# Split-heads rotary embedding in f32: two programs aligned in the instruction stream, one wait moved, one copy cut in two

## The chip, the cores and the metric

The kernel runs on one core of one Trainium2 chip. The metric is the device time of one execution in microseconds (us). Before the change it is 162.48 us, the median of six runs from 162.23 to 162.66.

The core has five instruction streams, each in order: TensorE (PE: matmuls; its weight loads are shown as PEld), VectorE (DVE), ScalarE (ACT), GpSimd (POOL) and SyncE (SP). In this kernel SP issues all loads and stores. They go through one hardware queue (q1) to 16 DMA engines, each of which works through its share of the packets in order. Instructions themselves are fetched from memory too: the page lists such packets as queue q14, kind "instruction".

## The reference

The input x has shape (16, 512, 1024), 16 heads of 64, all f32. Every head is split in two halves, which are rotated by the cosine and sine of their position:

```python
batch, seq, dim = x.shape
head_dim = dim // num_heads
half_dim = head_dim // 2
x = x.reshape(batch, seq, num_heads, head_dim)
x1, x2 = (x[..., :half_dim].copy(), x[..., half_dim:].copy())
cos = cos[None, :, None, :].copy()
sin = sin[None, :, None, :].copy()
rotated = np.concatenate([x1 * cos - x2 * sin, x1 * sin + x2 * cos], axis=-1)
```

So each output element is one input element times a cosine plus its partner in the other half times a signed sine. 33.6 MB are read and 33.6 MB written.

## The kernel before

**Tiles.** Two batches make one tile of 128 partitions: a partition holds 8 rows (sequence positions) of 1024 elements, so a tile is 4 MB, and there are 8 tiles. Five tile buffers (pool xp) exist. The result of a tile is written over its input and stored from there.

**Loads and stores.** SP issues, in this order: rows 0 to 2 of tile 0, the sine and cosine tables, rows 3 to 7 of tile 0, tiles 1 to 4, and four tiny loads into a tile named spare that nothing reads (line 92). Then come the stores as tiles are done; behind the store of tile 2 it issues the loads of tiles 5, 6 and 7 (line 74), which wait until their buffers have been stored. The last tile is stored in two halves: rows 0 to 3, and rows 4 to 7 (LAST_OUT).

**Setting up.** GpSimd makes an identity matrix. VectorE clears a tile (line 97) that three matmuls use to clear the PSUM accumulators own_ps and pe_ps, and copies two identities side by side (spread, line 109). Two matmuls by spread (lines 113 and 114) put the tables on all partitions, and VectorE makes the signed sine table sns (lines 116 and 117) and its copy for row 0 (line 119).

**The rows of a tile are computed in three ways.**
- Row 0 (ROW_OWN): VectorE puts x times cosine into PSUM (own_ps, cos_product, line 141; this is done at the end of the tile before). Then own_product (line 150) multiplies the row in place by the sine, TensorE adds it to own_ps with halves swapped (pe_add, line 176), and ScalarE copies own_ps back over the row (line 209).
- Row 3 (ROW_PE): GpSimd makes the sine product b3 (line 165); VectorE makes the cosine product in PSUM, half a row at a time (pe_ps, line 141); TensorE adds, and ScalarE copies back (pe_half, line 181).
- The pairs of rows (1, 2), (4, 5) and (6, 7): GpSimd makes the sine product of both rows into a buffer b (sin_rows and sin_product, line 165), VectorE the cosine product into PSUM (pd, line 141), and VectorE adds the two over the rows (pair_sum, line 189).

GpSimd's buffers b come from a pool of three.

**The order** is that of the program: within tc.manual_schedule() nothing is moved. The framework finds from the memory that instructions touch which ones need a semaphore wait; it leaves out a wait that an earlier instruction of the same engine has already had. An instruction that needs more waits than it can carry gets separate wait instructions ahead of it, shown as EVENT_SEMAPHORE. Of the three 128x2048 sums of a tile each has one such instruction before it (24 in all, 21 ns each): a wait for VectorE's own product, beside the wait for GpSimd's b that the sum itself carries. Line 150 carries no wait.

Of the kernel before, what the change touches and what calls it, by code (L numbers as in the profile page):

```python
# [10 lines left out]
ALU = mybir.AluOpType  # L11
# [6 lines left out]
ROW_OWN, ROW_PE = 0, 3  # L18
# [10 lines left out]
def kernel(  # L29
# [13 lines left out]
    nc = tc.nc  # L43
# [20 lines left out]
    pd = ctx.enter_context(tc.tile_pool(name="pd", bufs=1, space=bass.MemoryType.PSUM))  # L64

    ctx.enter_context(tc.manual_schedule())

    tiles = [None] * NT

    def load(t, lo=0, hi=KK):  # L70
        if tiles[t] is None:
            tiles[t] = xp.tile([P, F], FP32, name="xt")
        s = slice(lo * dim, hi * dim)
        nc.sync.dma_start(out=tiles[t][:, s], in_=x_v[t][:, s])  # L74
# [23 lines left out]
    own_ps = pe.tile([P, dim], FP32)  # L98
    pe_ps = pe.tile([P, BANK], FP32)
    for ps in (own_ps[:, :BANK], own_ps[:, BANK:], pe_ps):  # L100
# [9 lines left out]
        out=spread.rearrange("p (b q) -> p b q", b=NB),  # L110
        in_=bass.AP(tensor=eye.tensor, offset=eye.offset, ap=[eye.ap[0], [0, NB], [1, PB]]),
# [9 lines left out]
    def heads(r):  # L121
        return r.rearrange("p (h a j) -> p h a j", a=2, j=half)

    def swapped(r):
        n = r.shape[1] // hd
        return bass.AP(tensor=r.tensor, offset=r.offset + half, ap=[r.ap[0], [hd, n], [-half, 2], [1, half]])

    def rows(t, k, n=1):
        return tiles[t][:, k * dim : (k + n) * dim]

    def cos_product(out, r, k, n=1):

        c = cos_t[:, k * half : (k + n) * half]
        m = r.shape[1] // (n * half)
        if n == 1:
            cb = bass.AP(tensor=c.tensor, offset=c.offset, ap=[c.ap[0], [0, m], [1, half]])
            o, i = (z.rearrange("p (a j) -> p a j", j=half) for z in (out, r))
        else:
            cb = bass.AP(tensor=c.tensor, offset=c.offset, ap=[c.ap[0], [half, n], [0, m], [1, half]])
            o, i = (z.rearrange("p (k a j) -> p k a j", k=n, j=half) for z in (out, r))  # L140
        nc.vector.tensor_tensor(out=o, in0=i, in1=cb, op=ALU.mult)  # L141

    def own_product(r):

        s = bass.AP(
            tensor=own_t.tensor,
            offset=own_t.offset + half,
            ap=[own_t.ap[0], [0, nh], [-half, 2], [1, half]],
        )
        nc.vector.tensor_tensor(out=heads(r), in0=heads(r), in1=s, op=ALU.mult)  # L150

    def sin_product(out, r, k, n):
        s = sns[:, k : k + n].rearrange("p k a j -> p (k a j)")
        if n == 1:
            sb = bass.AP(tensor=s.tensor, offset=s.offset, ap=[s.ap[0], [0, nh], [1, hd]])
            o, i = heads(out), swapped(r)
        else:
            sb = bass.AP(tensor=s.tensor, offset=s.offset, ap=[s.ap[0], [hd, n], [0, nh], [1, hd]])
            o = out.rearrange("p (k h a j) -> p k h a j", k=n, a=2, j=half)
            i = bass.AP(  # L160
                tensor=r.tensor,
                offset=r.offset + half,
                ap=[r.ap[0], [dim, n], [hd, nh], [-half, 2], [1, half]],
            )
        nc.gpsimd.tensor_tensor(out=o, in0=i, in1=sb, op=ALU.mult)  # L165

    def sin_rows(t, k, n):
        b = bp.tile([P, 2 * dim], FP32, name="b")[:, : n * dim]
        sin_product(b, rows(t, k, n), k, n)
        return b  # L170

    def parts(r):
        return [r[:, i * BANK : (i + 1) * BANK] for i in range(r.shape[1] // BANK)]

    def pe_add(ps, other):
        nc.tensor.matmul(out=ps, lhsT=ident, rhs=other, start=False, stop=True, skip_group_check=True)  # L176

    def pe_half(k, r, b):
        cos_product(pe_ps, r, k)
        pe_add(pe_ps, b)  # L180
        nc.scalar.copy(out=r, in_=pe_ps)  # L181

    def pair_product(t, k):
        ps = pd.tile([P, 2 * dim], FP32, name="pd")
        cos_product(ps, rows(t, k, 2), k, 2)
        return ps, rows(t, k, 2)

    def pair_sum(ps, r, b):
        nc.vector.tensor_tensor(out=r, in0=ps, in1=b, op=ALU.add)  # L189

    def stores(t):
        lo = 0
        for hi in LAST_OUT if t == NT - 1 else (KK,):
            store(t, lo, hi)
            lo = hi
        if t + 1 == NT - BUFS:
            for n in range(BUFS, NT):
                load(n)

    cos_product(own_ps, rows(0, ROW_OWN), ROW_OWN)  # L200
    for t in range(NT):
        first, second, third = PAIRS
        b1 = sin_rows(t, first[0], 2)
        p1 = pair_product(t, first[0])
        r0 = rows(t, ROW_OWN)
        own_product(r0)
        for ps, r in zip(parts(own_ps), parts(r0)):
            pe_add(ps, swapped(r))
        nc.scalar.copy(out=r0, in_=own_ps)  # L209
        b3 = sin_rows(t, ROW_PE, 1)  # L210
        b2 = sin_rows(t, second[0], 2)
        pair_sum(*p1, b1)
        h0, h1 = zip(parts(rows(t, ROW_PE)), parts(b3))
        pe_half(ROW_PE, *h0)
        p2 = pair_product(t, second[0])
        b1 = sin_rows(t, third[0], 2)
        pair_sum(*p2, b2)
        pe_half(ROW_PE, *h1)
        p1 = pair_product(t, third[0])
        if t + 1 < NT:  # L220
            cos_product(own_ps, rows(t + 1, ROW_OWN), ROW_OWN)
        pair_sum(*p1, b1)
        stores(t)
# [35 lines left out]
```

## Time and profile before

| | |
|---|---|
| median of six runs | 162.48 us (162.23 to 162.66) |
| the profiled execution | 162.66 us |
| its span, first to last instruction | 160.9 us |
| PE busy | 58.6 us, 36% of the span |
| VectorE busy | 136.3 us, 85% |
| ScalarE busy | 18.4 us, 11% |
| GpSimd busy | 127.2 us, 79% |
| DMA | 67.25 MB, 418 GB/s over the span |
| granted TensorE clock, mean | 0.648 of full speed |

The groups of instructions that the change touches, with count and mean duration:

| line, engine | what | count | mean ns |
|---|---|---|---|
| 165 GpSimd | sine product of two rows, 128x2048 | 24 | 4527 |
| 165 GpSimd | sine product of one row, 128x1024 | 8 | 2356 |
| 150 VectorE | own product, 128x1024 | 8 | 1213 |
| 189 VectorE | sum of a pair, 128x2048 | 24 | 2287 |
| 209 ScalarE | copy of own_ps, 128x1024 | 8 | 1012 |
| 181 ScalarE | copy of pe_ps, 128x512 | 16 | 586 |

The share of busy time is an average over the whole span. Engines work at the same time, so busy times are not added up; what sets the end is read from the chain of waits, from what still runs in the last microseconds, and from who waits for whom. A start and a duration are in us of the span's own clock. The trace also holds one record for each DMA packet, with its start, duration, size and queue.

### The profile page before, as it was taken

To read this page: it belongs to the slowest core of one execution; us is meant where nothing else is said; L and a number is where in the kernel's file an instruction comes from. 1 tells how busy PE (TensorE), PEld (TensorE's weight loads), DVE (VectorE), ACT (ScalarE), POOL (GpSimd) and SP (SyncE) were. 2 spreads that over 40 slices of the span, in tenths; PEclk is the share of its full clock that TensorE was granted. 3 is DMA by queue.
4 is the path that set the end of the run, shared out by engine and by line. 5 is a ranking of instruction groups with operands and counts; after the bars stand their busy time and mean duration, and the time that the engine had idled before them with its cause. 6 is when DMAs were issued, how large, how long until landed. Compare 5 with 4: busy or idle time off the path is not lost.

```text
span 160.9 us, 443 instructions
## 1 busy us (share of the span) xinstructions
PE 58.6 (36%) x71; PEld 19.6 (12%) x71; DVE 136.3 (85%) x85; ACT 18.4 (11%) x25; POOL 127.2 (79%) x38
## 2 busy tenths in 40 slices
PE   3041915055503731191309250745047402922000
PEld 0111301021102210131003010211022101310000
DVE  1059969999999999999999999999999999998000
ACT  0001311003000301011100310031003010211000
POOL 1039999999999999988998899898999899840000
PEclk9999995558555775568555955585557655685555
DMA  5999999999999999999999999999999999999993
GB/s 192 394 423 457 416 489 399 391 505 407 391 505 408 391 424 489 391 399 505 401 399 489 407 399 497 407 399 489 407 399 497 407 399 497 407 399 444 399 444 155
DMA packets 2787, 67.25 MB, mean 418 GB/s; under 512 B 354, under 2 KB 482, under 8 KB 482
## 3 DMA queue, kind: packets, MB, share of 16 engines
q1 hardware_dynamic: 2786, 67.24, 97.8%
q14 instruction: 1, 0.01, 0.0%
HBM read 33.69 MB, written 33.55 MB: 418 GB/s over the span
## 4 chain that ended last, share of the span: by engine, by line
DVE 68%; issue 12%; POOL 6%; DMA 4%; PE 1%; SPq 0%; DVEq 0%
DVE xt L189 33%; DVE pd L141 31%; POOL b L165 6%; DMA b<-in_sin_dram 4%; DVE pe_ps L141 3%; PE tab L113 1%; PE tab L114 1%; DVE sns L116 0%; DVE xt L150 0%; DVE own_ps L141 0%; SPq L74 0%; DVE sns L117 0%; DVEq L189 0%
## 5 line engine op out<-in xcount | busy, mean ns | idle before, releaser
L165 POOL TENSOR_TENSOR b<-xt,sns 128x2048 f32<-128x2048 f32 (+1 forms) x32 | 126.5, 3984 | 14.7 <-DVE sns L117 9.3
L189 DVE TENSOR_TENSOR xt<-pd,b 128x2048 f32<-128x2048 f32 x24 | 54.9, 2287 | 2.4 <-POOL b L165 1.6
L141 DVE TENSOR_TENSOR pd<-xt,tab 128x2048 f32<-128x2048 f32 x24 | 55.0, 2292 | 0.2
L176 PE MATMUL own_ps<-xt,ident 128*128 128x512 f32 x32 | 30.2, 1099 | 54.0 <-DVE xt L150 48.3
L176 PE MATMUL pe_ps<-b,ident 128*128 128x512 f32 x32 | 26.6, 924 | 26.9 <-DVE pe_ps L141 26.9
L176 PEld LDWEIGHTS own_ps<-xt,ident 128*128 128x128 f32 x32 | 9.4, 324 | 74.0 <-DVE xt L150 59.3
L209 ACT COPY xt<-own_ps 128x1024 f32<-128x1024 f32 x8 | 8.1, 1012 | 73.3 <-PE own_ps L176 73.3
L176 PEld LDWEIGHTS pe_ps<-b,ident 128*128 128x128 f32 x32 | 8.8, 304 | 43.0 <-DVE pe_ps L141 34.4
L181 ACT COPY xt<-pe_ps 128x512 f32<-128x512 f32 x16 | 9.4, 586 | 39.3 <-PE pe_ps L176 39.2
L141 DVE TENSOR_TENSOR pe_ps<-xt,tab 128x512 f32<-128x512 f32 x16 | 10.9, 684 | 0.0
L141 DVE TENSOR_TENSOR own_ps<-xt,tab 128x1024 f32<-128x1024 f32 x8 | 9.8, 1222 | 0.0
L150 DVE TENSOR_TENSOR xt<-xt,tab 128x1024 f32<-128x1024 f32 x8 | 9.7, 1213 | 0.0
L116 DVE TENSOR_SCALAR sns<-tab 128x256 f32<-128x256 f32 x1 | 0.4, 425 | 8.2 <-PE tab L114 8.2
L209 ACT ACT_TABLE_LOAD x1 | 1.3, 1283 | 15.4 <-DVE xt L150 15.4
L113 PE MATMUL tab<-b,spread 64*128 64x256 f32 x2 | 1.2, 693 | 5.0 <-DMA b<-in_sin_dram 5.0
L101 PE MATMUL own_ps<-zero 128*128 128x512 bf16 x2 | 1.0, 620 | 1.2 <-DVE zero L97 1.2
L113 PEld LDWEIGHTS tab<-b,spread 64*128 64x128 f32 x2 | 0.5, 311 | 5.9 <-issue 5.9
L114 PE MATMUL tab<-b,spread 64*128 64x256 f32 x2 | 1.1, 628 | 0.0
L97 DVE MEMSET zero<- 128x256 uint32 x1 | 0.3, 272 | 0.9 <-PEq L240 0.9
L114 PEld LDWEIGHTS tab<-b,spread 64*128 64x128 f32 x2 | 0.7, 330 | 0.2
L101 PE MATMUL pe_ps<-zero 128*128 128x512 bf16 x1 | 0.6, 635 | 0.0
L101 PEld LDWEIGHTS <-zero 128*128 128x128 bf16 x3 | 0.3, 123 | 1.5 <-DVE zero L97 1.2
(9 smaller groups left out, 1.8 us busy)
## 6 DMA issues: line engine op xcount, KB each, us to landing
xt<-in_x_dram SPq DMA_DIRECT2D x7, 4096.0 KB, 29.7
out_dram<-xt SPq DMA_DIRECT2D x7, 4096.0 KB, 24.8
out_dram<-xt SPq DMA_DIRECT2D x2, 2048.0 KB, 10.3
xt<-in_x_dram SPq DMA_DIRECT2D x1, 2560.0 KB
xt<-in_x_dram SPq DMA_DIRECT2D x1, 1536.0 KB
b<-in_sin_dram SPq DMA_DIRECT2D x1, 64.0 KB
b<-in_cos_dram SPq DMA_DIRECT2D x1, 64.0 KB
spare<-in_sin_dram SPq DMA_DIRECT2D x1, 0.1 KB
```

Of the source, the lines that this page charges most:

```text
L97: nc.vector.memset(zero, 0.0)
L101: nc.tensor.matmul(out=ps, lhsT=zero[:, :P], rhs=zero, start=True, stop=True)
L113: nc.tensor.matmul(out=sin_t, lhsT=spread, rhs=sin_sb, start=True, stop=True)
L114: nc.tensor.matmul(out=cos_t, lhsT=spread, rhs=cos_sb, start=True, stop=True)
L116: nc.vector.tensor_scalar_mul(out=sns[:, :, 0, :], in0=sin_k, scalar1=-1.0)
L141: nc.vector.tensor_tensor(out=o, in0=i, in1=cb, op=ALU.mult)
L150: nc.vector.tensor_tensor(out=heads(r), in0=heads(r), in1=s, op=ALU.mult)
L165: nc.gpsimd.tensor_tensor(out=o, in0=i, in1=sb, op=ALU.mult)
L176: nc.tensor.matmul(out=ps, lhsT=ident, rhs=other, start=False, stop=True, skip_group_check=True)
L181: nc.scalar.copy(out=r, in_=pe_ps)
L189: nc.vector.tensor_tensor(out=r, in0=ps, in1=b, op=ALU.add)
L209: nc.scalar.copy(out=r0, in_=own_ps)
```

## The change

Three things are changed.

1. Right after the schedule is set to manual, VectorE and GpSimd each get an alignment directive, addr_align(128, max_nops=0). It is no operation of the engine: when the program is loaded, padding is put in so that the engine's next instruction lies at a multiple of 128 instruction slots. With max_nops=0 the padding is not executed; the loader puts a branch over it.
2. The sine product of the first pair of a tile (b1, GpSimd) and the own product of row 0 (line 150, VectorE) get an explicit dependency: the own product waits for b1. The helpers return their instructions for this. The first sum of the tile, which also needs b1 and comes later on VectorE, then needs no wait of its own for GpSimd.
3. ScalarE's copy of own_ps (1024 elements) becomes two copies of 512, each behind TensorE's matmul of that half in the program.

The products, sums and matmuls stay the same, and so do all loads and stores and their order.

```diff
     ctx.enter_context(tc.manual_schedule())
+    nc.vector.addr_align(128, max_nops=0)
+    nc.gpsimd.addr_align(128, max_nops=0)
...
-        nc.vector.tensor_tensor(out=heads(r), in0=heads(r), in1=s, op=ALU.mult)
+        return nc.vector.tensor_tensor(out=heads(r), in0=heads(r), in1=s, op=ALU.mult)
...
-        nc.gpsimd.tensor_tensor(out=o, in0=i, in1=sb, op=ALU.mult)
+        return nc.gpsimd.tensor_tensor(out=o, in0=i, in1=sb, op=ALU.mult)
 
     def sin_rows(t, k, n):
         b = bp.tile([P, 2 * dim], FP32, name="b")[:, : n * dim]
-        sin_product(b, rows(t, k, n), k, n)
-        return b
+        return b, sin_product(b, rows(t, k, n), k, n)
...
+    after = mybir.DependencyInfo(mybir.DependencyClass.Sync, mybir.DependencyReason.DATA)
     cos_product(own_ps, rows(0, ROW_OWN), ROW_OWN)
     for t in range(NT):
         first, second, third = PAIRS
-        b1 = sin_rows(t, first[0], 2)
+        b1, made = sin_rows(t, first[0], 2)
         p1 = pair_product(t, first[0])
         r0 = rows(t, ROW_OWN)
-        own_product(r0)
+        ins = own_product(r0)
+        tc.add_manual_dep(ins.ins, made.ins.name, after, reason="one wait for this and the sum")
         for ps, r in zip(parts(own_ps), parts(r0)):
             pe_add(ps, swapped(r))
-        nc.scalar.copy(out=r0, in_=own_ps)
-        b3 = sin_rows(t, ROW_PE, 1)
-        b2 = sin_rows(t, second[0], 2)
+            nc.scalar.copy(out=r, in_=ps)
+        b3, _ = sin_rows(t, ROW_PE, 1)
+        b2, _ = sin_rows(t, second[0], 2)
         pair_sum(*p1, b1)
...
-        b1 = sin_rows(t, third[0], 2)
+        b1, _ = sin_rows(t, third[0], 2)
```

## The prediction

> **What bounds the kernel now.** I read the chain of waits first, then the DMA part of the page, then the last microseconds in windows, then the single packet records of the trace.
>
> ```profile
> ## 4 chain that ended last, share of the span: by engine, by line
> DVE 68%; issue 12%; POOL 6%; DMA 4%; PE 1%; SPq 0%; DVEq 0%
> ```
>
> Taken alone, this says that VectorE (DVE) sets the end. The DMA part contradicts it:
>
> ```profile
> DMA packets 2787, 67.25 MB, mean 418 GB/s; under 512 B 354, under 2 KB 482, under 8 KB 482
> ## 3 DMA queue, kind: packets, MB, share of 16 engines
> q1 hardware_dynamic: 2786, 67.24, 97.8%
> q14 instruction: 1, 0.01, 0.0%
> ```
>
> The packets of the one data queue fill 97.8% of the time of all 16 DMA engines. VectorE's last instruction, the last sum (line 189), ends at 148.22 us of the timeline; the span is 160.86. The windows show what runs after it (columns: window, length, busy time of PE, PEld, DVE, ACT, POOL, granted clock, DMA share, GB/s):
>
> ```profile
> 148.00:152.00 4.00, 0.00 (x0) 0.00 (x0) 0.22 (x1) 0.00 (x0) 0.00 (x0) 0.50 0.90 385
> 152.00:156.00 4.00, 0.00 (x0) 0.00 (x0) 0.00 (x0) 0.00 (x0) 0.00 (x0) 0.50 0.99 422
> 156.00:158.00 2.00, 0.00 (x0) 0.00 (x0) 0.00 (x0) 0.00 (x0) 0.00 (x0) 0.50 1.09 467
> 158.00:159.00 1.00, 0.00 (x0) 0.00 (x0) 0.00 (x0) 0.00 (x0) 0.00 (x0) 0.50 0.20 82
> 159.00:160.00 1.00, 0.00 (x0) 0.00 (x0) 0.00 (x0) 0.00 (x0) 0.00 (x0) 0.50 0.04 16
> ```
>
> For twelve microseconds only DMA works, at full share until about 158, and then a ragged tail: a share of 0.20 of 16 engines is about three, 0.04 less than one. So the end is set by a DMA engine that finishes late. The packet records name it. A 32 KB packet takes 1.213 us and the next one of the same engine starts 0.004 before its end, so records can be strung into 16 rows, one per DMA engine. From 55 us on no row has a hole above 0.1 us. Twelve rows end between 158.30 and 158.54; the others at 158.74, 158.89, 159.31 and 159.69. From the last packet to the span's end are 160.86 - 159.69 = 1.17 us of completion and closing.
>
> Where did the last row get its 1.2 us? The page counts one instruction packet; asked for a narrow stretch, the DMA view places it:
>
> ```profile
> DMA packets 17, 0.53 MB, mean 532 GB/s; under 512 B 0, under 2 KB 0, under 8 KB 0
> q1 hardware_dynamic: 16, 0.52, 124.2%
> q14 instruction: 1, 0.01, 1.9%
> ```
>
> That is the stretch 79.5 to 80.5. The record: 8192 B at 79.862, 0.309 us. It sits in a row whose packet ended at 79.866; the row's next data packet starts at 80.168 and takes 1.595 instead of 1.213. Due at 79.862 + 1.213 = 81.075, it ends at 81.763: the fetch cost its row **0.69 us** and made it the latest. Its lateness against the median was 0.09 before and 0.78 after. The same row loses 0.36 more at 109.674 (a packet of 1.571, no fetch recorded there), which gives the 1.2 at the end. Queue and row continue without a hole, so nothing gives that time back.
>
> The alignment in the change is to 128 slots. VectorE has 123 recorded instructions and 64 of them were over at 79.86; GpSimd 62 and 36. An engine whose unrecorded opening is some 62 slots crosses a 128-slot line there, if it is VectorE. That is inference: the record does not name the engine. [...]
>
> **The change part by part.**
>
> *Alignment of VectorE.* Added: at most one branch over padding, after the opening barrier (0.66 us), ahead of the memset of line 97. Its body has 85 operations plus 32 stand-alone semaphore waits (35 recorded, three of them of barriers), 117; eight go (below): 109, with four at the end 113, under 128. So if VectorE makes the fetch at 79.86, it moves to the start. Removed there: 0.69 us of the last row, and 0.075 of the row beside it (its packet at 80.157 took 1.288). That leaves 159.69 - 0.69 = 159.00 for the first and 159.31 - 0.08 = 159.23 for the second, which becomes the end. **Gain 0.46 us.** The fetch then has to happen near 0.7 to 1.5. The first data packet of any row starts at 1.736, and the DMA view of 0 to 1.7 counts no packet, so ahead of 1.736 it is free: price 0. If it runs into the first loads, the nearest row is the one at 79.86: 0.69 per fetch, two fetches 1.38. I take 0, since about 1 us lies free and a fetch took 0.3; both ends stay in the range.
>
> *What waits behind the branch.* On VectorE the memset, which the zeroing matmuls need, and the copy to spread (line 109, over at 1.55); on GpSimd the identity, which spread waits for. All meet at the matmul of line 113, which waits for the sin load until 7.51. Cover: some 5.9 us. With that gone, the whole computation slides, and the next cover is that of the stores (below).
>
> *Alignment of GpSimd.* The same branch. Its 62 instructions do not reach 128 from a line, so no later fetch. Gain: 0 if it fetched nothing in the span; up to 0.36 on the last row if the stretch at 109.674 is its fetch. That row is no longer the end, so I take 0.
>
> [...] The record here is of 8 KiB, and its cost is not hidden but 0.69 us on the row that ends last. [...]
>
> *The own product waits for GpSimd's product.* Line 150 now waits for the first b1 of its tile, and the first sum (line 189) loses that wait, and with it one of its two semaphores: eight of VectorE's 24 waits of 21 ns ahead of line 189 go. From the instruction records, b1 of tile 1 ends at 30.84 and line 150 starts at 32.56; the margins of tiles 1 to 7 are 1.73, 2.96 and then 3.76. Only tile 0 waits:
>
> ```profile
> 14.11 1.21 DVE L150 TENSOR_TENSOR xt<-xt,tab 128x1024 f32<-128x1024 f32 x1
> 15.25 2.28 DVE L189 TENSOR_TENSOR xt<-pd,b 128x2048 f32<-128x2048 f32 x1
> 17.45 0.68 DVE L141 TENSOR_TENSOR pe_ps<-xt,tab 128x512 f32<-128x512 f32 x1
> 18.04 2.29 DVE L141 TENSOR_TENSOR pd<-xt,tab 128x2048 f32<-128x2048 f32 x1
> 21.91 2.29 DVE L189 TENSOR_TENSOR xt<-pd,b 128x2048 f32<-128x2048 f32 x1 [1.58 <-POOL b L165]
> ```
>
> GpSimd's b1 ends at 15.07, so line 150 starts near 15.15 instead of 14.11, and what is queued behind it on VectorE (sum, pe_ps, pd) slides 1.05. The second sum waits for GpSimd's b2 anyway, 1.58 idle: 0.53 are left over. TensorE's own matmuls and ScalarE's copy slide 1 us too; the store of tile 0 needs them at 30.4. On the path: 0. In the other tiles, consecutive operations start 0.07 to 0.10 before the end of the one ahead, with or without a satisfied wait, so the dropped wait is worth at most 8 x 0.03 = 0.24 on VectorE, and nothing at the end.
>
> *ScalarE's copy of line 209 in two.* 16 x 0.585 - 8 x 1.012 = 1.26 us more busy, on an engine that is busy 18.4 of 160.9. It frees own_ps by halves; the next user is a product 5 us later (copy over at 38.64, product at 43.88). Path: 0.
>
> *The cover of all this.* VectorE's timing enters the end only through the stores. The store of the last tile's first four rows is issued at 146.40; packets come about 1.0 us after an issue (0.73 to 1.736 for the first load), and the rows finish the store ahead of it at 148.6. So 1.2 us of slack, 4.2 for the last store, and 6 or more for every earlier one (the least are store 2, issued at 64.34, its turn at 71.5, and store 6, 132.24 and 139.3). VectorE must slip by more than 1.2 us at the end before the time moves, and each microsecond beyond costs one.
>
> **Sum.** Span 160.86 - 0.46 = 160.40. The profiled execution's time is 162.66, 0.18 above the median of the six runs (162.48). Taken from the median: 162.48 - 0.46 = **162.0 us**. A run of this kernel can tell about 0.2%, 0.33 us, from no change.
>
> **The rivals.**
>
> *A. The fetch is moved, not saved.* It, or another engine's, still falls into the loads and costs its row 0.69. For: 0.3 to 0.5 us (the records before the span take 0.31 to 0.55) must fit ahead of 1.736, behind a branch not before 0.66. Against: one fetch fits. Time: 162.48, within 0.2.
>
> [...]
>
> *C. Larger gain.* The row ending at 159.31 has dozens of packets that are 5 to 30 ns long, a drift that no instruction explains; if it belongs to this one execution, and the stretch at 109.674 goes as well, the end falls to the fourth row, 158.74: gain 0.95, 161.5.
>
> *D. The wait on line 150 hurts.* It needs 1.2 us on VectorE at the end, against margins of 3.76: I give it nothing of its own.
>
> **Chances.** Forecast (161.8 to 162.2) 0.47, A 0.22, B 0.17, C 0.14. Faster by over 0.2% (below 162.15): 0.47 + 0.14 = 0.61; within 0.2%: 0.22; slower: 0.17. The forecast's own range stands in brackets; the range of 8 in 10 takes in A whole, half of C and the mild end of B: 161.6 to 162.8.
>
> **What would show it.** No instruction packet between 2 and 158 us, one or more before 1.74; no data packet of 1.5 us or more near 80; the last packet near 159.2 and the windows after 158 emptier; line 150 of tile 0 near 15.15 and the second sum still near 21.9; 16 stand-alone waits at the sums instead of 24. Wrong would be: an instruction packet still in mid-run (another engine's, or VectorE's body is longer than I count), or a last row that is late from its first load on. VectorE's end at 148.2 may move by 0.3 either way without meaning anything.

## The result, and the profile after

The changed kernel takes 163.34 us (median of 20 runs, 162.53 to 164.05) against 162.43 us before (41 runs beside them): a ratio of 1.005, 95% interval 1.0039 to 1.0061. It is slower by some 0.9 us, where 162.0 and a gain were forecast. Its runs also spread over 1.5 us; most of those before lie within 0.6.

The page of the changed kernel, the parts on DMA and on the chain of waits:

```profile
DMA packets 2788, 67.26 MB, mean 417 GB/s; under 512 B 354, under 2 KB 482, under 8 KB 482
q1 hardware_dynamic: 2786, 67.24, 97.8%
q14 instruction: 2, 0.02, 0.1%
...
DVE 70%; issue 10%; POOL 6%; DMA 5%; PE 1%; SPq 0%; DVEq 0%
```

The data packets are the same. There are now two instruction packets instead of one, and the chain again names VectorE, which again is not what ends last. Both packets lie at the start: 8192 B at 1.735 us, 1.193 us long, and 8192 B at 3.228, 0.407 long. None is left in mid-run. The stretch from 1.6 to 2.0 us in the DMA view:

```profile
q1 hardware_dynamic: 8, 0.10, 136.0%
q14 instruction: 1, 0.01, 18.6%
```

The fetch starts together with the first data packets (the first of those at 1.746). GpSimd's branch is recorded at 0.693, so 1.04 us pass from the branch to the packet; SyncE's first load needs the same 1.0 (0.73 to 1.746). The free time ahead of 1.736 was not reached.

VectorE's branch is recorded at 0.761, and its packet starts 2.47 us later. Neither engine waits for its packet: the instruction behind VectorE's branch, the memset, and the one behind GpSimd's start before either packet does. The first instruction of each in the kernel before, then in the changed one:

```profile
0.85 0.27 DVE L97 MEMSET zero<- 128x256 uint32 x1 [0.85 <-PEq L240]
0.73 0.20 POOL masks.py:197 MEMSET ident<- 128x128 f32 x1 [0.29 <-POOLq L240]
```

```profile
1.42 0.27 DVE L99 MEMSET zero<- 128x256 uint32 x1 [1.42 <-PEq L243]
1.14 0.20 POOL masks.py:197 MEMSET ident<- 128x128 f32 x1 [0.70 <-POOLq L243]
```

SyncE's issues in the timeline (start, duration, line, operation), first of the kernel before, then of the changed one:

```profile
1.16 0.53 SPq L84 DMA_DIRECT2D b<-in_sin_dram  x1
1.74 0.58 SPq L85 DMA_DIRECT2D b<-in_cos_dram  x1
2.36 2.62 SPq L74 DMA_DIRECT2D xt<-in_x_dram  x5
```

```profile
1.17 0.53 SPq L86 DMA_DIRECT2D b<-in_sin_dram  x1
1.75 1.31 SPq L87 DMA_DIRECT2D b<-in_cos_dram  x1
3.10 2.65 SPq L76 DMA_DIRECT2D xt<-in_x_dram  x5
```

The issue of the cosine table takes 1.31 us instead of 0.58; it ends just after the fetch does (3.06 and 2.93). The load of rows 3 to 7 of tile 0, which SyncE issues next, is issued 0.74 us later than before, and the loads behind it some 0.8. The windows of both kernels from 6 to 8 us (before, then after; the last column is GB/s) show the DMA engines at the passage from the first load to this one:

```profile
6.00:8.00 2.00, 0.35 (x1) 0.38 (x2) 0.00 (x0) 0.00 (x0) 0.00 (x0) 1.00 1.13 398
```

```profile
6.00:8.00 2.00, 0.00 (x0) 0.00 (x0) 0.00 (x0) 0.00 (x0) 0.00 (x0) 1.00 1.18 309
```

The engines look busy in both (share over 1), but less data starts: the first 16 packets of the load take 1.37 us on average instead of 1.06. Strung into rows as in the prediction, all 16 rows are late after it. The landing records of each DMA give the lateness of the median row and, on top of it, of the last row, in us:

| DMA that lands | before: median row | last row beyond it | after: median row | last row beyond it |
|---|---|---|---|---|
| rows 3 to 7 of tile 0 | 13.41 | 0.31 | 14.02 | 0.77 |
| tile 4 | 52.33 | 0.25 | 52.91 | 0.74 |
| store of tile 1 | 71.69 | 0.43 | 72.26 | 0.80 |
| tile 5 | 91.03 | 0.90 | 91.68 | 0.69 |
| store of tile 3 | 120.16 | 1.11 | 120.81 | 0.81 |
| last store | 158.83 | 1.20 | 159.45 | 0.91 |

Read it by columns. The step that was to be saved is saved: before, the last row falls back from 0.43 to 0.90 at the fetch of 79.9; after, it does not. But all rows are 0.6 late from rows 3 to 7 on, and the last one 0.8 more. At the end 0.62 is lost and 0.29 won: the span grows by 0.33, to 161.2. This execution (162.98) lies 0.36 below the median of its kernel. Of the 0.9 us the first profile shows 0.3; a second one below shows 0.5.

The windows at the end of the changed kernel:

```profile
156.00:158.00 2.00, 0.00 (x0) 0.00 (x0) 0.00 (x0) 0.00 (x0) 0.00 (x0) 0.50 1.03 442
158.00:159.00 1.00, 0.00 (x0) 0.00 (x0) 0.00 (x0) 0.00 (x0) 0.00 (x0) 0.50 0.77 328
159.00:160.00 1.00, 0.00 (x0) 0.00 (x0) 0.00 (x0) 0.00 (x0) 0.00 (x0) 0.50 0.08 33
```

From 158 to 159 the share is 0.77 (before 0.20): the body of rows ends later, not one row.

### The profile page after: what moved, and what is told of

It is laid out like the page before. It is cut to its first block, busy times and chain, and to the rows that moved or that the text cites. A ratio compares the mean times of both kernels' runs of the same rounds, so it can differ in the third digit from the quotient of the medians.

```text
span 161.2 us, 450 instructions
## 1 busy us (share of the span) xinstructions
PE 66.0 (41%) x71; PEld 18.7 (12%) x71; DVE 136.4 (85%) x85; ACT 20.0 (12%) x33; POOL 127.1 (79%) x38
## 4 chain that ended last, share of the span: by engine, by line
DVE 70%; issue 10%; POOL 6%; DMA 5%; PE 1%; SPq 0%; DVEq 0%
DVE xt L190 32%; DVE pd L143 26%; POOL b L167 6%; DVE pe_ps L143 6%; DVE xt L152 5%; DMA b<-in_sin_dram 5%; PE tab L115 1%; PE tab L116 1%; DVE sns L118 0%; DVE own_ps L143 0%; SPq L76 0%; DVE sns L119 0%; DVEq L190 0%
## 5 line engine op out<-in xcount | busy, mean ns | idle before, releaser
L177 PE MATMUL own_ps<-xt,ident 128*128 128x512 f32 x32 | 33.2, 1140 | 61.5 <-DVE xt L152 55.9
L177 PE MATMUL pe_ps<-b,ident 128*128 128x512 f32 x32 | 31.0, 1070 | 12.1 <-DVE pe_ps L143 12.1
L212 ACT COPY xt<-own_ps 128x512 f32<-128x512 f32 x16 | 9.4, 585 | 87.2 <-PE own_ps L177 87.2
L177 PEld LDWEIGHTS own_ps<-xt,ident 128*128 128x128 f32 x32 | 8.0, 312 | 85.0 <-DVE xt L152 66.9
```

Of the source, the lines that this page charges most:

```text
L212: nc.scalar.copy(out=r, in_=ps)
```

## The experiments

Ratios are to the kernel before, timed on the same chip beside them. Edits are shown in excerpts. "Lateness" is that of the last row beyond the median row.

**The parts of the change.** First without the alignments:

```diff
-    nc.vector.addr_align(128, max_nops=0)
-    nc.gpsimd.addr_align(128, max_nops=0)
```

> The changed kernel without the two alignments: moved wait and split copy stay. If the alignments cost the 0.9 us (their two fetches run into the first loads), this is within 0.2% of before (162.3 to 162.6), with one instruction packet in mid-run and none between 1 and 4 us. If the moved wait or the split copy costs it, the time stays near 163.3. A shift of the mid-run fetch tells whose it is: VectorE has one wait fewer per tile, so its fetch comes some 4 slots (4 to 6 us) later than 79.86; GpSimd has one wait more per tile, so its fetch would come earlier.

Measured: 163.15 us, ratio 1.005 (1.0038 to 1.0062). This is as slow as the whole change. The profile has VectorE's fetch at 82.18 (later, as expected if it is VectorE's, but by 2.3 us and not by 4 to 6), with 0.325 us and a next packet of 1.875: 0.99 lost on its row instead of 0.69. And the closing, the time from the last packet to the end of the span, is 1.50 us instead of 1.17. The expectation had neither the longer closing nor the dearer fetch; the next two runs take the parts singly. The moved wait alone:

```diff
-        own_product(r0)
+        ins = own_product(r0)
+        tc.add_manual_dep(ins.ins, made.ins.name, after, reason="one wait for this and the sum")
```

> The kernel before with the moved wait alone (no alignment, one copy of own_ps). If the moved wait is what cost 0.7 us in the kernel without alignments, by eight more waits on GpSimd that push its closing over a line (0.33 in the closing) and by a later and dearer fetch of VectorE (at 82 instead of 80), this is again 162.9 to 163.3, with 1.50 us from the last packet to the end of the span instead of 1.17. If the split copy did it: 162.3 to 162.6 and 1.17.

Measured: 163.15 us, ratio 1.0041 (1.0027 to 1.0055), the fetch at 82.35, the closing 1.53. How the moved wait reaches the closing is seen by GpSimd's wait instructions; the view of GpSimd's product in the kernel before and in the changed one:

```profile
L165 POOLq EVENT_SEMAPHORE  x9: 17/17/43, 7.2 to 120.9; - x9
```

```profile
L167 POOLq EVENT_SEMAPHORE  x17: 17/17/43, 8.1 to 138.9; - x17
```

Eight more. GpSimd's product for the third pair of a tile writes into the buffer that the one for the first pair filled. Before, it waited for VectorE's first sum, which itself had waited for GpSimd: that covered both. Now the sum no longer waits for GpSimd, so the framework gives the product for the third pair a second wait, on GpSimd itself. The closing instructions of the program, on GpSimd, in the kernel before and in the moved wait alone:

```profile
L254 POOLq EVENT_SEMAPHORE  x4: 17/17/17, 160.2 to 160.8; - x4
```

```profile
L255 POOLq EVENT_SEMAPHORE  x4: 17/17/17, 160.7 to 161.7; - x4
```

The same four take 0.6 us before and 1.0 here: between GpSimd's last DRAIN and the next of the four, 0.43 us pass instead of 0.08. In both kernels with the eight waits and without GpSimd's alignment, an instruction packet of 8192 B follows some 0.5 us behind the end of the span. I read this as GpSimd's program crossing a line in the closing barrier, for which all engines wait (the last of the closing waits starts on each of the five at 161.7 here, at 160.8 before); the run with GpSimd's alignment and the same eight waits, below, tests it. The split copy alone:

```diff
             pe_add(ps, swapped(r))
-        nc.scalar.copy(out=r0, in_=own_ps)
+            nc.scalar.copy(out=r, in_=ps)
```

> The kernel before with the split copy alone. ScalarE is idle for 140 us: same, 162.3 to 162.6, the fetch still near 79.9, the closing 1.17. If the split costs something, up to 163.1.

Measured: 162.86 us, ratio 1.002 (1.001 to 1.0029): not the same, though ScalarE is nowhere late. VectorE's separate wait instructions fall by four (those at its products of lines 141 and 150: 8 and 0 before, 1 and 3 here), and the fetch comes at 82.26, with a next packet of 1.779: 0.88 on the row instead of 0.69. That fits the 0.3 us; that it is the cause was not shown by itself.

The alignments alone:

```diff
     ctx.enter_context(tc.manual_schedule())
+    nc.vector.addr_align(128, max_nops=0)
+    nc.gpsimd.addr_align(128, max_nops=0)
```

> The kernel before with both alignments and nothing else. If the alignments are the cause: near the changed kernel, 163.0 to 163.6, two instruction packets near 1.7 and 3.2 us, SyncE's third issue (the cosine table) near 1.3 us long instead of 0.58. If the cost comes from the rest of the change: 162.0 to 162.6.

Measured: 163.78 us, ratio 1.008 (1.0067 to 1.0093): the cost is there without the rest. Packets at 1.757 (1.080 us) and 3.335 (0.429), the cosine issue 1.224 long, the median row 0.63 late at rows 3 to 7. VectorE's alignment alone:

```diff
+    nc.vector.addr_align(128, max_nops=0)
```

> The kernel before with VectorE's alignment alone. If the fetch at 79.86 is VectorE's, no instruction packet is left in mid-run and one is at 1.7 us; one early fetch instead of two should cost about half of the 0.9: 162.7 to 163.1, if each fetch costs alike; near 162.4 if only the second of the two, or GpSimd's, does harm.

Measured: 164.31 us, ratio 1.0119 (1.0104 to 1.0135), the slowest of the parts. Its one instruction packet, in the stretch 3 to 5 us, and SyncE's issue of the cosine table:

```profile
q14 instruction: 1, 0.01, 1.0%
```

```profile
1.75 0.58 SPq L86 DMA_DIRECT2D b<-in_cos_dram  x1
```

The packet starts at 3.913, 3.15 us behind VectorE's branch (0.762). No fetch is left in mid-run, so the one at 79.86 is VectorE's. The cosine issue is not stalled, and the median row is only 0.2 late. But one row is 1.12 late from the second load on, 1.37 at 52 us and 2.10 at the end. GpSimd's alignment alone:

```diff
+    nc.gpsimd.addr_align(128, max_nops=0)
```

> The kernel before with GpSimd's alignment alone. If the fetch at 79.86 is VectorE's, it stays, and an early one is added: the loss of one early fetch with no gain, 162.8 to 163.2, at least as slow as with VectorE's alignment alone. If the mid-run fetch is GpSimd's, it goes, and the time lies below that of VectorE's alignment alone.

Measured: 162.67 us, ratio 1.0012 (0.9999 to 1.0025). SyncE's issue, and the instruction packet in the stretch 79.5 to 81:

```profile
1.74 1.38 SPq L86 DMA_DIRECT2D b<-in_cos_dram  x1
```

```profile
q14 instruction: 1, 0.01, 1.3%
```

VectorE's fetch stays (80.33). GpSimd's is the early one at 1.73, 1.249 long; the issue beside it is the long one, and in the median of the runs it costs little by itself (the profiled run, 163.08, is the slowest of the twelve). The prices don't add: 1.9 and 0.2 us apart, 1.3 together (0.85 the second time, below). Why VectorE's fetch alone is dearer than both together is not shown. The change without VectorE's alignment, so this against the changed kernel:

```diff
-    nc.vector.addr_align(128, max_nops=0)
```

> The changed kernel without VectorE's alignment: moved wait, split copy and GpSimd's alignment. The closing should be back at 1.17 (GpSimd no longer crosses a line there, worth 0.33), one early fetch near 1.73 (GpSimd's) and VectorE's fetch near 82 should be there. If GpSimd's early fetch costs little (its alignment alone measured 162.67 against 162.46), this is 162.7 to 163.1, below both the changed kernel and the one without alignments; if each early fetch costs as VectorE's does, 163.3 or more.

Measured: 162.74 us, ratio 1.0018 (1.0005 to 1.003), the closing at 1.18, as expected, although the eight waits are there: GpSimd's alignment pays for them. It is faster than the whole change, though compared across two chips. What the two fetches do to the loads is read from the landing of tile 1, the first whole tile (us):

| kernel | fetches before 5 us | median row | last row beyond it | last row |
|---|---|---|---|---|
| before | none | 23.12 | 0.31 | 23.43 |
| moved wait alone, split copy alone | none | 23.21, 23.23 | 0.19, 0.14 | 23.40, 23.37 |
| GpSimd aligned | GpSimd's | 23.38 | 0.50 | 23.87 |
| all but VectorE's alignment | GpSimd's | 23.54 | 0.33 | 23.87 |
| VectorE aligned | VectorE's | 23.29 | 1.12 | 24.41 |
| both aligned, first and second time | both | 23.74, 23.34 | 0.84, 1.18 | 24.58, 24.52 |
| changed kernel, first and second time | both | 23.72, 23.54 | 0.79, 1.17 | 24.51, 24.71 |

Against the kernel before, the last column falls into three groups: GpSimd's fetch costs the last row some 0.45 us, VectorE's 1.0, both together 1.1 to 1.3. The profiles without an early fetch, those of other runs here included, lie between 23.24 and 23.58, so each of these prices is known to some 0.2 either way. How that is shared out between all rows and one row differs between two executions of the same kernel (0.84 and 1.18 beyond the median). In the kernel with GpSimd aligned and in that with all but VectorE's alignment, the fetch at 80 to 82 us comes on top later.

**Does the place of VectorE's fetch set its price?** An offset moves it. By my count of slots the branch then stays within its line, and I took it to bring no fetch at the start:

```diff
     ctx.enter_context(tc.manual_schedule())
+    nc.vector.addr_align(128, offset=102, max_nops=0)
```

> The kernel before, with VectorE's program aligned to slot 102 of a line instead of slot 0, and GpSimd's not aligned. By the count of slots VectorE's program begins near slot 62, so the branch stays within its line and triggers no fetch at the start; the line ends 26 slots later, so the fetch comes near 30 us, in the midst of loads, instead of at 79.86, next to the change from stores to loads. If it is the place that makes it dear, it costs its row 0.3 instead of 0.7: 162.0 to 162.3. If any branch in the program brings an early fetch: one instruction packet before 5 us and 163 or more. If a fetch costs the same wherever it falls: 162.3 to 162.6.

Measured: 163.65 us, ratio 1.0077 (1.0056 to 1.0097). The stretch 36.8 to 37.8 of its DMA view holds the only instruction packet of the run:

```profile
q14 instruction: 1, 0.01, 2.0%
```

So the count of slots was right (of VectorE's recorded instructions behind the branch, 26 are over at the fetch, and the line had 26 slots left), though the time was taken 7 us too early, and this branch brought no fetch at the start: the one packet is at 37.12. The price was not: 0.325 us and a next packet of 1.876, together 0.99, in the midst of loads. The row is 0.88 late then, 1.25 at 52 us, 1.32 before 110 and 1.96 after. With another offset:

```diff
+    nc.vector.addr_align(128, offset=83, max_nops=0)
```

> The kernel before with VectorE aligned to slot 83: by 14 slots a tile the fetch comes near 60 us. If a late row loses more at each later change between loads and stores (50, 81, 109 us), the time lies between the fetch at 37 (163.65) and at 80 (162.45): 162.7 to 163.4, the row 0.7 to 1.0 late after the fetch and 1.4 or more after 110. If only the fetch itself counts, the time does not depend on its place: 163.4 to 163.9, or 162.3 to 162.6.

Measured: 162.48 us, ratio 0.9997 (0.9982 to 1.0011), the fetch at 60.45 (45 instructions over, 45 slots left in the line), 0.78 on its row, lateness 0.84 after it and 1.00 at the end. That is neither of the two expectations as they stood: the place matters, but a fetch at 60 costs no more than at 80. Over the profiles:

| kernel | VectorE's fetch at | packet + stretch of the next | lateness at tile 4 (52) | at tile 6 (101) | at the end | time |
|---|---|---|---|---|---|---|
| VectorE aligned | 3.91 | 0.84 | 1.37 | 1.35 | 2.10 | 164.31 |
| offset 102 | 37.12 | 0.99 | 1.25 | 1.32 | 1.96 | 163.65 |
| offset 83 | 60.45 | 0.78 | 0.25 | 0.92 | 1.00 | 162.48 |
| before | 79.86 | 0.69 | 0.25 | 0.91 | 1.20 | 162.43 |
| split copy alone | 82.26 | 0.88 | 0.24 | 0.89 | 1.13 | 162.86 |
| moved wait alone | 82.35 | 0.89 | 0.22 | 1.00 | 1.60 | 163.15 |

The fetch itself sets its row back by about the same at 4 us (0.84; 0.84 to 1.19 in the four profiles with both engines aligned and the loads in their usual order) as at 37, 60, 80 or 82 (0.69 to 0.99). What differs is what follows. At 50 us the queue passes from loads to stores, and there the rows of the first two kernels fall back again, by 0.25 and 0.38; at the next such passage, at 110, those two and the moved wait alone lose 0.5 to 0.7 more. Not every late row does: in the changed kernel's second profile, below, the lateness is 1.18 before and 1.15 after the passage at 50, and still 1.19 at 110, while in the second profile of the two alignments alone it grows from 1.19 to 1.67 at 50. What decides is open.

**Why are all rows late at the start?** One tiny load ahead of the load of rows 3 to 7 delays its issue without any fetch:

```diff
+    spare = fixed.tile([16, len(EXTRA), 16], FP32)
+    nc.sync.dma_start(out=spare[:EXTRA[0], 0], in_=sin_v[:EXTRA[0], :16])
     for lo, hi in zip(FIRST, FIRST[1:]):
         load(0, lo, hi)
...
-    spare = fixed.tile([16, len(EXTRA), 16], FP32)
-    for i, n in enumerate(EXTRA):
+    for i, n in list(enumerate(EXTRA))[1:]:
```

> The kernel before, with the first of the four tiny loads moved ahead of the load of rows 3 to 7 of tile 0, so that SyncE issues that load some 0.55 us later; no alignment. If the late issue of this load alone makes all DMA rows late (the 0.6 us at the landing of rows 3 to 7 in the changed kernel), the median row lands it 0.3 to 0.6 us later than 13.41 and the time is 162.7 to 163.1. If the rows are late because of the early instruction fetch itself, nothing moves: 162.3 to 162.6.

Measured: 162.37 us, ratio 1.0 (0.9989 to 1.0011), the median row at 13.38. With two of them, the load is issued at 3.22, later than the 3.10 of the changed kernel:

```diff
+    spare = fixed.tile([16, len(EXTRA), 16], FP32)
+    for i, n in list(enumerate(EXTRA))[:2]:
+        nc.sync.dma_start(out=spare[:n, i], in_=sin_v[:n, :16])
     for lo, hi in zip(FIRST, FIRST[1:]):
...
-    spare = fixed.tile([16, len(EXTRA), 16], FP32)
-    for i, n in enumerate(EXTRA):
+    for i, n in list(enumerate(EXTRA))[2:]:
```

> The kernel before with two of the four tiny loads ahead of the load of rows 3 to 7 of tile 0, so that this load is issued some 1.1 us later, as late as in the changed kernel; no alignment, no early fetch. If the late issue makes all rows late beyond some point, the median row lands at 13.7 to 14.1 instead of 13.41 and the time is 162.7 to 163.2. If the early fetch is needed for it: 13.4 and 162.3 to 162.6.

Measured: 162.65 us, ratio 1.001 (0.9996 to 1.0024), the median row at 13.37. The late issue by itself makes no row late; the reading that it is the cause falls with it. Then the other order, in the changed kernel: first the tables on another queue,

```diff
-    nc.sync.dma_start(out=sin_sb, in_=sin_v)
-    nc.sync.dma_start(out=cos_sb, in_=cos_v)
+    nc.scalar.dma_start(out=sin_sb, in_=sin_v)
+    nc.scalar.dma_start(out=cos_sb, in_=cos_v)
```

> The changed kernel with the two table loads issued by ScalarE's queue instead of SyncE's, so that the load of rows 3 to 7 is SyncE's second issue, ahead of the fetch at 1.7 us. If the stalled issue is what makes all rows late, the median row is back at 13.4 and the time falls by 0.3 to 0.6 against the changed kernel, to 162.6 to 163.0; the row with the fetch stays late. If the fetch itself makes all rows late, the time stays at 163.1 to 163.6.

Measured: 163.82 us, ratio 1.0084 (1.0062 to 1.0105). The median row is at 13.41, as without any fetch, and tile 1's last row at 23.81 instead of 24.5, while both fetches are there (1.765 and 3.151). The issue beside the fetch is now that of tile 1, and it is the long one (1.21 us, 0.43 in the control below); tile 2 is issued behind it, at 2.89. Neither is late in the median row (23.10 and 32.80, in the control 23.20 and 32.92). The total was no measure: the cosine table landed at 12.27 instead of 7.85, VectorE's work behind it started 3.8 later, and the last stores waited for it. Its control, the same edit in the kernel before:

> The kernel before with the two table loads issued by ScalarE's queue; no alignment. It is the control for the changed kernel with the same edit. The load of rows 3 to 7 is issued 1.2 us earlier than before. If the start of that load is late already in the kernel before (its first packets took 1.05 us against 0.77 later), this gains up to 0.3: 162.1 to 162.4; if not, it stays within 0.2% of before.

Measured: 163.38 us, ratio 1.0063 (1.0045 to 1.0081). No gain from the earlier load (median row 13.50), and the same slide: the last store lands at 160.8 in the median row instead of 158.8. Second, the load ahead of the tables on the same queue:

```diff
+    for lo, hi in zip(FIRST, FIRST[1:]):
+        load(0, lo, hi)
...
     nc.sync.dma_start(out=sin_sb, in_=sin_v)
     nc.sync.dma_start(out=cos_sb, in_=cos_v)
-    for lo, hi in zip(FIRST, FIRST[1:]):
-        load(0, lo, hi)
```

> The changed kernel with the load of rows 3 to 7 of tile 0 issued ahead of the two table loads, on the same queue. The tables land some 6 us later and the computation with them, so the time itself is no measure (165 or more, the last stores waiting for VectorE). What counts is the median row at the landing of rows 3 to 7, which has 0.13 MB less ahead of it (some 0.3 us): 13.1 to 13.2 if only a load issued behind the fetch suffers, 13.6 or more if the early fetches slow all rows whatever the order.

Measured: 166.48 us, ratio 1.0255 (1.0231 to 1.0279), as much the slide as anything. The load of rows 3 to 7 lands at 12.92 in the median row, not late; what is now behind the fetch is: tile 1 lands at 23.46 instead of 23.12, its last row at 24.56. So a late issue alone costs the median row nothing, and a fetch under way costs it something only for some loads. In the changed kernel's first profile some 0.25 of the 0.6 are there at the landing of rows 0 to 2 already (6.89 against 6.64), a load issued ahead of the fetch. The rest is lost at the load queued right behind the two tables, rows 3 to 7 there and tile 1 in this last run; with the tables on another queue no load is late against its control. Whether it is the tables that make the difference was not tested, and how all 16 engines are slowed stays open.

**The changed kernel again, and the alignments alone, on one chip,** without a further edit:

> The changed kernel, unchanged, beside the next one. 163.2 to 163.5 as measured; its profile should show again two early fetches, all rows some 0.6 us late at rows 3 to 7 of tile 0, no fetch in mid-run.

> The two alignments alone, beside the changed kernel on the same chip. If the moved wait and the split copy give nothing under the alignments, both agree within 0.2%; if the 0.4 us between them was real, this one is again 0.3 to 0.5 us slower than the changed kernel.

Measured: 163.33 us, ratio 1.0053 (1.0036 to 1.007), and 163.41, 1.0065 (1.0045 to 1.0084). The difference of 0.4 between the two did not come back. Under the alignments the moved wait and the split copy change nothing that these runs can tell. The second profile of the changed kernel has the median row 0.42 late at rows 3 to 7 and 0.45 at the end, the last row 1.22 beyond it, and a span of 161.3. The second of the alignments alone has the median row 0.22 late there and the last row 1.67 beyond it at the end, span 161.6.

No version that ran beats the kernel before by more than its measurement can tell.

## Why the prediction was wrong

- **DMA sets the end, by the row that is last:** right. In the profiles the span ends 1.16 to 1.18 us after the last row's last packet, whichever row that is, or 1.50 to 1.53 where GpSimd's closing is longer. Where VectorE was made later (tables on ScalarE), the stores came late and all rows ended together (in the control, the kernel before with that edit, the span of 161.8 ends 1.0 behind the landing of the last store in the median row, before 2.0).
- **The fetch at 79.86 is VectorE's, costs its row 0.69, and the alignment takes it away:** right, shown by the two alignments taken singly. That a line has 128 slots was an inference; with offsets 102 and 83 the fetch came when 26 and 45 recorded instructions were over, 128 less the offset. In the first profile after, the last row no longer falls back there: its lateness goes from 0.80 at the store of tile 1 to 0.69 at tile 5, before from 0.43 to 0.90.
- **"I take 0, since about 1 us lies free and a fetch took 0.3":** this step failed. It counted the free time from the branch and gave the fetch no latency. GpSimd's packet starts 1.04 us behind its branch (0.693 to 1.735), as the first load's does behind its issue, so it starts together with the loads. The trace of before had that latency (0.73 to 1.736 for the first load), and I used it for the stores only. VectorE's packet, the dearer one, starts later still, 2.47 us behind its branch in the changed kernel and 3.15 with VectorE aligned alone, in the midst of the loads; no number of the trace of before foretold that, and what sets this delay is not shown. In place of 0, GpSimd's fetch holds back its row's first data packet to 2.92, by which time the others are at their second (0.46 us), and VectorE's costs its row 0.84 (a packet of 0.41 and a next one of 0.89 instead of 0.46). At the landing of tile 1 the last row is 0.45 later with GpSimd's fetch and 1.0 with VectorE's.
- **The upper bound of 0.69 a fetch, on one row:** too small, and it did not stay in the range: two such fetches, 1.38, on the row left at 159.23 end at 160.61, 0.92 behind the 159.69 of before, which makes 163.4, above the range's 162.8. VectorE's early fetch cost its row 0.84, and with GpSimd's, and the loads in their usual order, the median row was 0.2 to 0.6 later than before at rows 3 to 7 (the kernels without an early fetch differ by 0.15 there). Nothing in the trace of before showed the second.
- **Slower, given 0.17,** is what came: two programs, each with one early fetch into the first loads (at 1.735 and 3.228 us). With every such fetch the last row of the first loads was later (by 0.45 to 1.3 us at the landing of tile 1), and partly all rows. Rival A's argument "one fetch fits" was wrong for the reason above.
- **The own product's wait and its covers:** right where it was costed. Line 150 is line 152 now:

```profile
16.18 1.22 DVE L152 TENSOR_TENSOR xt<-xt,tab 128x1024 f32<-128x1024 f32 x1 [0.90 <-POOL b L167]
17.32 2.28 DVE L190 TENSOR_TENSOR xt<-pd,b 128x2048 f32<-128x2048 f32 x1
22.97 2.29 DVE L190 TENSOR_TENSOR xt<-pd,b 128x2048 f32<-128x2048 f32 x1 [0.57 <-POOL b L167]
```

  The whole tile is 1.06 later than before, since the sine table lands at 8.59 instead of 7.51. Beyond that, the wait is 0.90, and 0.57 of idle time is left before the second sum (0.53 were forecast).
- **The cover of 1.2 us at the stores** was nearly used up by those 1.06 us: VectorE ends at 149.28, and the last stores are issued 1.06 later (1.27 in the second profile, where the rows are late too). In the profiles of the changed kernel it still held (from the landing of tile 6's store to that of the last store, the median row takes 9.68 and 9.70, before 9.70); whether it gives way in its slower runs is not known.
- **"GpSimd's alignment: 0", and "the dropped wait is worth nothing at the end":** wrong as a pair. The moved wait adds eight waits on GpSimd, which cost 0.33 to 0.36 us in the closing unless GpSimd is aligned. I counted the waits that VectorE loses and not those that the framework must add elsewhere: the sums lose eight (24 to 16), as forecast, but four come back on VectorE at the own product, and eight on GpSimd.
- **What waits behind the branch** was covered, as forecast: VectorE's memset starts at 1.42 after a branch to another line, at 1.06 after one within its line (offset 102), at 0.85 without, and the sine table lands at 8.59 only. But what VectorE waits for there is not the packet in the trace, which starts at 3.228; and that packet sets back a row of the loads, by 0.84.

## What to carry to other kernels

- Where DMA is the bound, as here, one instruction fetch need not be free: in mid-run it set one of 16 rows back by 0.7 to 1.0 us, and the span ended 1.16 to 1.18 us behind the last row's last packet (1.50 to 1.53 with the longer closing). Ask where the fetch goes, not only whether it is avoided. VectorE's at 4 and 37 us was dearer in the end (163.65 to 164.31) than at 60 or 80 (162.4 to 162.5), since its row fell back again later.
- Adding or removing a few wait instructions moved such a fetch (from 79.86 to between 82.18 and 82.35 us) and, as the runs here are read, pushed another engine's program over a line in the closing barrier (0.33 to 0.36 us). A wait taken from one instruction may come back on another engine whose order it had carried (eight waits on GpSimd here).
- Before a gap is called free, measure how long the thing takes to arrive there. The latency of the first load, 1.0 us, was in the trace, and for GpSimd's fetch it was the right one (1.04).

## What the runs showed of the hardware that was not expected

- Behind an instruction packet of 8192 B that took 0.31 to 0.33 us in mid-run, the next data packet of its row (1.213 us otherwise) was longer by 0.35 to 0.66: by 0.35 to 0.38 at 79 to 80 us, where stores pass to loads, 0.47 in the midst of stores (60 us), 0.57 to 0.66 in the midst of loads (37 and 82 us).
- In all eight profiles with GpSimd's alignment, SyncE's DMA issue beside the instruction fetch of 1.7 us took 1.2 to 1.4 us (the cosine table's 0.58 without that fetch).
- The instruction behind a branch to another line started before the instruction packet did: VectorE's at 1.42 with packets at 3.2 and 3.9, GpSimd's at 1.14 with its packet at 1.735.
- The stretched packet at 109.67 that the prediction could not explain has no fetch behind it: packets of 1.5 to 2.1 us stand there in kernels whose fetch is elsewhere (1.84 with the moved wait alone, 2.08 with VectorE aligned, 2.06 with offset 102), where the queue passes from loads to stores.
